# Matmul with batch norm on one core: a seventh raw row block, a fixed order of the tasks, and gamma's negation on GpSimd

## The chip, the cores and the metric

One core of a Trainium2 chip runs the kernel. The metric is the device time of one execution in microseconds, the median over several runs. The core has a matmul engine (TensorE, PE), a vector engine (VectorE, DVE), a scalar engine (ScalarE, ACT), a general engine (GpSimd, POOL) and a queue engine (SyncE, SP) that issues transfers. Each engine takes its own instructions in order, and they wait for each other through semaphores.

## The reference

```python
batch, m, k, n = 16, 512, 1024, 768
y = np.matmul(x, weight)                          # 8192 rows x 768 columns, all float32
mean = np.mean(y, axis=(0, 1), keepdims=True)     # per column
var = np.var(y, axis=(0, 1), keepdims=True)
y_norm = (y - mean) / np.sqrt(var + eps)
return (gamma * y_norm + beta).astype(np.float32)
```

Every output needs the mean and the variance of its column over all 8192 rows. So nothing of a column can be stored before all of its rows have been multiplied.

## The kernel before

The 8192 rows are cut into 16 chunks of 512 rows (`c`, C = 16), the 768 columns into 6 tiles of 128 (`nt`, NT = 6). x comes in through GpSimd's transfer queue as bfloat16 (L403), is turned by VectorE's 32x32 transposes (L428, L435), and for some chunks is also copied into a plain layout `x_pl` by ScalarE or VectorE (L547).

The first two column tiles are computed with rows on the partitions (L510, and L814 for the last two chunks). Their statistics are sums of the values and of the squares (L659 to L672), merged at L795 and L800 and summed over the partitions by a small matmul (L871). Their output is written in rows: VectorE multiplies (L937), GpSimd or VectorE adds the shift (L942), SP stores (L946). Chunks 14 and 15 of these tiles go through a TensorE transpose (L1074) instead.

The other four tiles are computed with columns on the partitions (L575, and L753 for the last chunk of the last tile). A unit is a matmul group over half of the depth, four matmuls; two units fill one of the eight banks of PSUM. The bank is free when VectorE has taken its statistics (L711) and ScalarE has copied it to SBUF (L715). For the third tile (nt = 2) ScalarE makes both sums itself from chunk 4 on (L720, L724). When a tile has all of its chunks, it is finished: total on ScalarE (nt = 2 alone, L980 to L986), variance on VectorE (L976), root on ScalarE (L990), then scale and shift per column (for nt = 2 L1001 on VectorE and L1004 to L1006 on ScalarE, with the negated gamma; for others L993 to L997).

An output block is two chunks of a tile, 1024 rows x 128 columns. Since it lies with columns on the partitions, it must be turned. There are three ways:

- `xact` (tiles 2 and 3): normalise in place (L1023 on ScalarE for nt = 2, L1026 on VectorE for nt = 3), transpose by a DMA that SP issues (L1220), convert to float32 on ScalarE (L1232), store (L1202).
- `pe` (tile 4): normalise, transpose on TensorE (L1044, single transposes put between the matmuls of later units), copy out on ScalarE (L1210), store (L1202).
- raw: the block is transposed by DMA before its statistics are known (L1106), and finished in rows: the scale and shift columns are spread along the rows (L1141, L1142 on VectorE, L1145 on GpSimd or ScalarE, L1158 on ScalarE), VectorE multiplies (L1174), GpSimd adds (L1178), SP stores (L1182). `RAW` names these blocks by tile and first chunk. Blocks of chunks 0 to 3 are transposed right behind the last load of x, ahead of the first store; the others later.

The last tile's 16 chunks are normalised on VectorE (L1348), transposed on TensorE (L1044), copied by ScalarE (L1361) and stored (L1364) after everything else. Their scale comes from L1308 to L1324. The first chunk is split into two quarters of a block for its stores.

The order of all this is made by a planner when the program is built. Each piece of work is a `Task` with a due time, the engines it may run on with assumed durations, what it depends on, and which buffers it takes or uses. `arrange` (L122) keeps a clock for each engine, takes the engine that can begin first, and gives it the ready task with the earliest due time. A unit of four matmuls may host single transposes of a block. Buffers are placed in the same pass, so the order also decides which earlier use a buffer has to wait for. The tasks are then emitted in that order, which fixes the order of instructions on each engine.

```python
RAW = {2:(0,2),3:(0,),4:(0,2,4)}                        # of L278
seq(nc.vector.tensor_scalar(ngamma, gamma_sb, -1.0, None, op0=ALU.mult))     # L964
ng = task(S, dve(0.1), negate_gamma, [affine, sr], True)                     # L966
```

Of the kernel before, what the change touches and what calls it, by code (L numbers as in the profile page):

```python
# [97 lines left out]
class Wires:  # L98
# [8 lines left out]
    def ready(self, queue):  # L107
        lanes = self.lanes[queue]
        return 0.0 if len(lanes) < self.LANES else lanes[-self.LANES]
# [9 lines left out]
        return t, land  # L119


def arrange(tasks, turns, log=None):  # L122

    free = {e: 1.25 for e in ("PE", "DVE", "ACT", "POOL", "SP")}
    wires = Wires()
    port = {"DVE": 0.0, "POOL": 0.0}
    left = sorted(tasks, key=lambda t: t.prio)
    order = []  # L130
    SEM, LOOK = 0.06, 0.2

    def ready(t):
        if t.after is not None and t.after.end is None:
            return None
        r = 0.0
        for d in t.deps:
            if d.end is None:
                return None
            r = max(r, d.end + SEM + t.slack)  # L140
        kept = [(s.pool, s.pool.mark()) for s in t.takes] if len(t.takes) > 1 else []
        fits = True
        for s in t.takes:
            p = s.pool.place(s)
            if p is None:
                fits = False
                break
            r = max(r, p[0] + SEM)
            if kept:
                s.pool.take(s, p[1])  # L150
        for pool, mark in reversed(kept):
            pool.reset(mark)
        if not fits:
            return None
        if t.dma:
            r = max(r, wires.ready(list(t.engines)[0]))
        return r

    def start_of(t, r, e):

        b = max(r, free[e])
        if e == "DVE" and t.lock:
            b = max(b, port["POOL"])
        elif e == "POOL" and not t.dma:
            b = max(b, port["DVE"])
        return b

    while left:
        seen = [(t, ready(t)) for t in left]
        first = {}  # L170
        for t, r in seen:
            if r is not None:
                for e in t.engines:
                    b = start_of(t, r, e)
                    if e not in first or b < first[e]:
                        first[e] = b
        if not first:
            raise RuntimeError(f"nothing can begin: {[(t.prio, t.emit) for t in left[:8]]}")
        e = min(first, key=lambda k: first[k])
        best = None  # L180
        for t, r in seen:
            if r is not None and e in t.engines and start_of(t, r, e) <= first[e] + max(LOOK, t.look):
                if best is None or t.prio < best[1]:
                    best = start_of(t, r, e), t.prio, t
        start, _, t = best
        for s in t.takes:
            s.pool.take(s, s.pool.place(s)[1])
        occ, lat = t.engines[e]
        t.hosted = []
        if t.hosts:  # L190
            room = t.hosts
            for u, r in seen:
                if u in turns and r is not None and r <= start + 0.3 and room >= 1:
                    n = min(room, turns[u][0])
                    if turns[u][0] == turns[u][1]:
                        places = [s.pool.place(s) for s in u.takes]
                        if any(p is None or p[0] > start for p in places):
                            continue
                        for s in u.takes:
                            s.pool.take(s, s.pool.place(s)[1])  # L200
                        u.takes_done, u.takes = u.takes, []
                    t.hosted.append((u, n))
                    turns[u][0] -= n
                    room -= n
                    occ += 0.0555 * n
                    lat += 0.0555 * n
        if t in turns:
            occ = lat = 0.0555 * turns[t][0]
            lat += 0.2
            t.count = turns[t][0]  # L210
        free[e] = start + occ
        if e == "DVE" and t.lock or e == "POOL" and not t.dma:
            port[e] = start + occ
        t.end = start + lat
        if t.dma:
            free[e], t.end = wires.send(e, start, occ, t.dma, t.count)
        t.start, t.engine = start, e
        order.append(t)
        left.remove(t)
        for u, n in t.hosted:  # L220
            if turns[u][0] == 0:
                u.end = t.end + 0.2
                left.remove(u)
    return order


# [1 line left out]
def kernel(  # L228
# [9 lines left out]
    nc = tc.nc  # L238
# [3 lines left out]
    ALU = mybir.AluOpType  # L242
# [5 lines left out]
    P = 128  # L248
# [26 lines left out]
    PARTED, LATE, SINGLE = (4,5,7,8,9,10), (12,13,14,15), (2,3,6)  # L275
    MODE = {2:'xact',3:'xact',4:('pe',)*8}
    MODE = {nt: m if isinstance(m, tuple) else (m,) * (C // GY) for nt, m in MODE.items()}
    RAW, RAWADD, RAWDUE = {2:(0,2),3:(0,),4:(0,2,4)}, {2:'POOL',3:'POOL',4:'POOL'}, {2:14.0,3:8.0,4:8.0}  # L278
    RING = 3 * CH // 32 * KQ // 2
    ENG = {"ACT": nc.scalar, "DVE": nc.vector, "POOL": nc.gpsimd, "SP": nc.sync}  # L280

# [11 lines left out]
    def seq(bi):  # L293

        ins = bi.ins
        prev = last.get(ins.engine)
        if prev is not None:
            tc.add_manual_dep(
                ins, prev,
                mybir.DependencyInfo(mybir.DependencyClass.NoSync, mybir.DependencyReason.DATA),  # L300
                reason="order",
            )
        last[ins.engine] = ins.name
        return bi

    gamma_sb = singles.tile([P, NT], f32)
# [28 lines left out]
    ngamma = singles.tile([P, NT], f32)  # L335
# [17 lines left out]
    tasks, turns = [], {}  # L353
    banks, xts, ys, sqs, rings = Pool(8), Pool(XT), Pool(YB), Pool(SQ), Space(RING)

    def task(prio, engines, emit, deps=(), lock=False, **kw):
        t = Task(prio, engines, emit, deps, **kw)
        t.lock = lock
        tasks.append(t)
        return t  # L360

    def dve(occ):
        return {"DVE": (occ, occ + 0.09)}
# [4 lines left out]
    def pool(occ):  # L368
        return {"POOL": (occ, occ + 0.05)}
# [70 lines left out]
    order = [("x", 0), ("w", 0, 2), ("x", 1), ("w", 2, 4)]  # L440
# [5 lines left out]
    t = 1.0  # L446
    affine = None
# [237 lines left out]
    def y_of(nt, c):  # L685
        return y_col.setdefault((nt, c // GY), Slot(ys))
# [174 lines left out]
    S = clock[0]  # L861
# [61 lines left out]
    sr = task(U + 0.1, dve(0.35), shift_rows, [sc], True)  # L923
# [32 lines left out]
    k = 0  # L956
# [4 lines left out]


    def negate_gamma(eng):
        seq(nc.vector.tensor_scalar(ngamma, gamma_sb, -1.0, None, op0=ALU.mult))  # L964

    ng = task(S, dve(0.1), negate_gamma, [affine, sr], True)  # L966

    def finish_tasks(nt):
        deps = [col_end[nt, c][0] for c in range(C)]
# [61 lines left out]
    def turn_block(prio, nt, m0, count, deps, uses):  # L1031

        bank = Slot(banks)
        todo = []

        def step():
            if not todo:
                o_ps = psum.tile([P, count, P], bf16, tag="b")
                bank.tile = o_ps
                for s in range(count):  # L1040
                    c, i = divmod(m0 // P + s, RT)
                    todo.append((o_ps[:, s], y(nt, c)[:, i * P:(i + 1) * P]))
            dst, src = todo.pop(0)
            seq(nc.tensor.transpose(dst, src, ident))  # L1044

        def emit(eng):
            for _ in range(emit.task.count):
                step()

        emit.step = step  # L1050
        t = task(prio, pe(0.0555 * count), emit, deps, takes=[bank], uses=uses)
        emit.task = t
        turns[t] = [count, count]
        return t, bank
# [213 lines left out]
    for nt in range(GA, NT - 1):  # L1268
# [10 lines left out]
        f = finish_tasks(nt)  # L1279
        start = clock[0] + 3.0  # L1280
# [58 lines left out]
    for c, r0, rows in ends:  # L1339
        due = E + 2.0 + 0.6 * c  # L1340
        n = max(rows // CH, 1)
# [13 lines left out]
        b, bank = turn_block(due + 0.6 * (n - 1), nt, m0, count, norms, [y_of(nt, c + i) for i in range(n)])  # L1355
# [7 lines left out]
        def store(eng, slot=slot, m0=m0, count=count):  # L1363
# [6 lines left out]
             uses=[slot])  # L1370

    order = arrange(tasks, turns)
    if "PLAN" in globals():
        PLAN.append(order)
# [37 lines left out]
```

## Time and profile before

| what | value |
|---|---|
| median of 3 runs | 206.29 us (206.23 to 206.86) |
| profiled execution, span from first to last instruction | 204.1 us |
| mean granted TensorE clock | 0.979 |
| first matmul on data (L510) | 12.14 us |
| last matmul of the last tile (L753), end in the chain of waits | 186.6 us |
| first transpose of a raw block issued (L1106) | 100.08 us |
| first store issued (L946) | 109.10 us |
| first store of the last tile issued (L1364) | 189.31 us |
| eleven stores of the last tile, issue from the first to the end of the last | 10.56 us |
| L1174, raw product on VectorE | 6, mean 1.21 us |
| L1178, raw sum on GpSimd | 6, mean 2.48 us |
| L1232, conversion on ScalarE | 13, mean 1.06 us |
| L1220, DMA transpose, on SP's queue | 13, median 1.70 us |
| L964, gamma's negation on VectorE | 1, 0.164 us |

A row of the groups gives line, engine, operation, written and read tile with the shape, the count, the busy time, the mean of one instruction in ns, and the idle time of the engine before it with what ended it. In a line of the timeline stand start, duration, engine, line and operation. In a line of the windows stand, after the stretch, its length, then the busy time and the count for PE, weight loads, DVE, ACT and POOL, then the granted clock, the DMA share and GB/s. A line of the waits has the waiting instruction, what ended the wait, the sum in us, how often, and the longest.

### The profile page before, as it was taken

Reading aid. Unit: us, or ns where it says so; the run is one execution under the profiler, and the core shown is the slowest. Engines: PE = TensorE matmul, PEld = TensorE weight load, DVE = VectorE, ACT = ScalarE, POOL = GpSimd, SP = SyncE. Lnnn points to the kernel's source line nnn. Section 1 sums busy time; section 2 is a strip of 40 time slices with the busy share of each in tenths; the row PEclk is TensorE's granted clock in tenths of the full one; section 3 lists DMA queues with packets and bytes.
Section 4 is the critical chain, followed back from the end, with each engine's and each line's share of the span. In section 5 each row is a group of like instructions: output and inputs, shape, how many; then the busy total and the mean of one; then the engine's idle time right before and its main releaser. Section 6 shows DMA issues by size and latency. Waiting matters only on the chain.

```text
span 204.1 us, 3510 instructions
## 1 busy us (share of the span) xinstructions
PE 189.3 (93%) x1210; PEld 114.5 (56%) x1210; DVE 159.3 (78%) x250; ACT 146.2 (72%) x260; POOL 124.1 (61%) x150
## 2 busy tenths in 40 slices
PE   7969999999999999999999999999999999997900
PEld 3457554657488888777865444444444445544600
DVE  4031879999999999969989998987999878657900
ACT  2001461368989999899978766999998959956950
POOL 7776954877499989997403999389613312940000
PEclk9999999999999999999999999999999999999965
DMA  4999999999999999999686899899999999999998
GB/s 71 172 199 196 176 196 196 196 197 197 190 193 197 197 196 196 196 197 195 103 181 200 297 339 336 248 301 328 295 322 227 336 303 274 347 343 310 310 347 253
DMA packets 98562, 48.74 MB, mean 239 GB/s; under 512 B 24304, under 2 KB 98032, under 8 KB 98544
## 3 DMA queue, kind: packets, MB, share of 16 engines
q0 software_dynamic: 34624, 18.36, 65.5%
q1 hardware_dynamic: 63920, 30.16, 52.6%
q8 instruction: 9, 0.15, 0.3%
q14 instruction: 9, 0.07, 0.1%
HBM read 36.71 MB, written 25.17 MB: 303 GB/s over the span
## 4 chain that ended last, share of the span: by engine, by line
PE 86%; ACT 3%; DMA 3%; POOL 2%; issue 1%; ACTq 0%; DVE 0%; POOLq 0%
PE y_ps L575 54%; PE y_ps L510 24%; PE y_ps L814 4%; ACT o_sb L1361 3%; DMA ring<-in_x_dram 3%; PE o_ps L1044 1%; POOL ring L403 1%; POOL w_sb L387 1%; PE y_ps L753 1%; PE a_ps L903 1%; PE o_ps L1074 0%; ACTq L1407 0%; PE idle_ps L591 0%; PE tot_ps L871 0%; ACT ring L1252 0%
## 5 line engine op out<-in xcount | busy, mean ns | idle before, releaser
L575 PEld LDWEIGHTS <-w_sb 128*128 128x128 bf16 x520 | 50.3, 97 | 57.6
L575 PE MATMUL y_ps<-xT_sb,w_sb 128*128 128x512 bf16 (+1 forms) x272 | 59.3, 371 | 0.0
L575 PE MATMUL y_ps<-x_pl,w_sb 128*128 128x512 bf16 x248 | 57.4, 379 | 0.0
L403 POOL DMA_DIRECT2D ring<-in_x_dram x76 | 47.2, 626 | 14.4 <-DMA ring<-in_x_dram 5.5
L510 PE MATMUL y_ps<-w_sb,xT_sb 128*128 128x256 bf16 x448 | 50.6, 273 | 1.7 <-DMA ring<-in_x_dram 1.6
L510 PEld LDWEIGHTS <-xT_sb 128*128 128x128 bf16 x448 | 43.5, 98 | 9.4 <-DVE xT_sb L435 2.9
L435 DVE STREAM_TRANSPOSE xT_sb<-ring 128x1024 f32<-128x1024 f32 (+1 forms) x29 | 31.2, 1111 | 14.1 <-DMA ring<-in_x_dram 13.9
L711 DVE BATCH_NORM_STATS2 stats<-y_ps 128x6 f32<-128x512 f32 x46 | 30.9, 687 | 7.7 <-PE y_ps L575 7.2
L715 ACT CAST y_sb<-y_ps 128x512 bf16<-128x512 f32 x51 | 29.0, 593 | 10.4 <-DVE stats L711 6.3
L547 ACT COPY x_pl<-xT_sb 128x1024 bf16<-128x1024 bf16 x32 | 32.8, 1063 | 1.7 <-DVE xT_sb L435 1.7
L942 POOL TENSOR_TENSOR ring<-ring,sum 128x1024 f32<-128x1024 f32 (+1 forms) x11 | 23.8, 2188 | 14.9 <-ACT y_ps L724 10.9
L659 ACT ACTIVATE sq_sb<-y_ps 128x512 f32<-128x512 f32 x28 | 16.3, 610 | 16.2 <-PE y_ps L510 15.9
L666 POOL TENSOR_TENSOR sum<-sum,sq_sb 128x512 f32<-128x512 f32 x20 | 25.6, 1278 | 3.0 <-ACT sq_sb L659 1.7
L662 DVE TENSOR_TENSOR sum<-y_ps,sum 128x512 f32<-128x512 f32 x28 | 18.9, 675 | 6.3 <-ACT sq_sb L659 5.3
L672 ACT CAST y_sb<-y_ps 128x512 bf16<-128x512 f32 x28 | 16.3, 594 | 8.2 <-DVE sum L662 8.0
L1178 POOL TENSOR_TENSOR ring<-ring,sum 128x1024 f32<-128x1024 f32 x6 | 14.8, 2477 | 9.8 <-issue 8.5
L937 DVE TENSOR_TENSOR ring<-y_sb,a_ps 128x1024 f32<-128x1024 bf16 (+1 forms) x16 | 16.7, 1079 | 0.1
L1044 PE MATMUL o_ps<-ident,y_sb 128*128 128x128 bf16 x104 | 13.1, 221 | 1.6 <-DVE y_sb L1348 1.5
L1232 ACT CAST ring<-ring 128x1024 f32<-128x1024 bf16 x13 | 13.8, 1063 | 0.6 <-DMA ring<-y_sb 0.6
L1145 POOL COPY sum<-sum 32x256 f32<-32x256 f32 (+1 forms) x17 | 5.8, 340 | 13.4 <-DVE sum L1142 6.5
L428 DVE STREAM_TRANSPOSE xT_sb<-ring 128x2048 bf16<-128x2048 bf16 x6 | 13.5, 2290 | 0.1
L591 PE MATMUL idle_ps<-idle_sb 128*128 128x512 f32 x18 | 9.6, 688 | 1.5 <-DVE idle_sb L316 1.5
(104 smaller groups left out, 153.7 us busy)
## 6 DMA issues: line engine op xcount, KB each, us to landing
out_dram<-ring SPq DMA_DIRECT2D x37, 512.0 KB, 3.4
ring<-in_x_dram POOLq DMA_DIRECT2D x52, 256.0 KB, 8.8
out_dram<-o_sb SPq DMA_DIRECT2D x6, 512.0 KB, 4.7
ring<-in_x_dram POOLq DMA_DIRECT2D x16, 128.0 KB, 5.9
w_sb<-in_weight_dram POOLq DMA_DIRECT2D x8, 192.0 KB, 6.2
out_dram<-ring SPq DMA_DIRECT2D x6, 256.0 KB, 3.0
ring<-in_x_dram POOLq DMA_DIRECT2D x4, 192.0 KB, 7.8
out_dram<-o_sb SPq DMA_DIRECT2D x3, 256.0 KB, 2.5
```

The lines of the kernel that those rows point to most:

```text
L403: bi = seq(nc.gpsimd.dma_start(x_bf[32 * i:32 * i + 32], src[:, :, KQ * i:KQ * (i + 1)]))
L435: seq(nc.vector.transpose(dst, src[:, :, jw0:jw1]))
L510: seq(nc.tensor.matmul(y_ps[:, s], x_of(c, jw, e, t * P, (t + 1) * P), w_sb[:, jw, e, 0:NA], start=(s == 0 and jw == 0 and e == 0), stop=( ...
L547: seq(nc.scalar.copy(dst, pairs) if eng == "ACT" else ENG[eng].tensor_copy(dst, pairs))
L575: seq(nc.tensor.matmul(y_ps, w_sb[:, jw, e, nt * P:(nt + 1) * P], moving(c, jw, e, q0 * QR, q1 * QR, parted), start=(jw == 0 and e == 0 an ...
L659: seq(nc.scalar.activation(sq_sb[:, 0:n], slot.tile[:, 0:n], AF.Square))
L662: seq(nc.vector.tensor_add(sum1, slot.tile[:, 0:n], sum1))
L666: seq(ENG[eng].tensor_add(acc, acc, state["sq"][:, 0:n]))
L711: seq(nc.vector.bn_stats(dst, slot.tile))
L715: seq(nc.scalar.copy(y(nt, c), slot.tile))
L937: seq(nc.vector.tensor_mul(slot.o, y_row[c].y[:, s0:s1], aff[0][:, None, :].to_broadcast([P, n, NA])))
L942: seq(ENG[eng].tensor_add(slot.o, slot.o, row[:, None, :].to_broadcast([P, n, NA])))
```

## The change

1. `RAW` gets block (3, 2): the rows of chunks 2 and 3 of the fourth column tile are now transposed raw and finished in rows, as (3, 0) was before.
2. The planner no longer chooses. A table `ORDER` names every task by its number in the order of creation, with the letter of its engine (P, V, A, G, S), and after a plus sign the blocks whose transposes a matmul unit hosts and how many of each. `arrange` walks the table, keeps its clocks for the placing of buffers, and raises an error when a task is not ready.
3. Gamma's negation runs on GpSimd, and depends on the load of gamma alone.

```diff
+ORDER = (
+    "G0 P59 G3 G8 A9 G4 G7 V1 V2 P60 G10 P61 P62 P63 P64 P65 V5 V6 P66 G12 P67 P68 P69 P70 P71 G14 P76 A72 "
...
+    "V643 V657 V683 V661 V675 V644 G645 G646 P685+658.4 P686+658.4 P689+662.4 P690+662.3 P678+662.1 A684 "
...
+    "A760 A775 S739 S766 S771 S743 S781 S776 S761 "
+)
...
-    left = sorted(tasks, key=lambda t: t.prio)
+    left = tasks
...
-    while left:
-        seen = [(t, ready(t)) for t in left]
...
-        e = min(first, key=lambda k: first[k])
...
+    NAMES = {"P": "PE", "V": "DVE", "A": "ACT", "G": "POOL", "S": "SP"}
+    for word in ORDER.split():
+        word, _, riders = word.partition("+")
+        t, e = left[int(word[1:])], NAMES[word[0]]
+        r = ready(t)
+        if r is None:
+            raise RuntimeError(f"out of order: {word}")
+        start = start_of(t, r, e)
...
+        for rider in riders.split(",") if riders else ():
+            i, n = rider.split(".")
+            u, n = left[int(i)], int(n)
...
-    RAW, RAWADD, RAWDUE = {2:(0,2),3:(0,),4:(0,2,4)}, {2:'POOL',3:'POOL',4:'POOL'}, {2:14.0,3:8.0,4:8.0}
+    RAW, RAWADD, RAWDUE = {2:(0, 2),3:(0, 2),4:(0, 2, 4)}, {2:'POOL',3:'POOL',4:'POOL'}, {2:14.0,3:8.0,4:8.0}
...
     def negate_gamma(eng):
-        seq(nc.vector.tensor_scalar(ngamma, gamma_sb, -1.0, None, op0=ALU.mult))
-
-    ng = task(S, dve(0.1), negate_gamma, [affine, sr], True)
+        seq(nc.gpsimd.tensor_scalar(ngamma, gamma_sb, -1.0, None, op0=ALU.mult))
+
+    ng = task(S, pool(0.3), negate_gamma, [affine])
```

What the table makes of the order, read from the two built programs:

- Up to the last chunk of x the engines' orders agree; the first differences stand where the row sums are merged (L795, L871).
- SP issues six raw transposes ahead of the first store instead of five, then the row stores and those of chunks 14 and 15 alternate.
- TensorE has the same matmuls and transposes. Eight column matmuls stand between the transpose blocks of chunks 14 and 15 that stood behind them; units of different chunks alternate more often; the hosted transposes are spread otherwise.
- At the finish of the third tile VectorE runs three L937 ahead of the aggregate L976 (two and an L711 before), then the spreading copies L1141, L1142 and one more L937 ahead of the next L711, and ScalarE runs the root, L1004 to L1006 and three L1023 ahead of the first L715 of the next tile. Before, one L715 stood ahead of the root, and one behind each L1023.
- GpSimd runs the negation behind the first two L942, the copies L1318 to L1320 behind the last L942, and the four small copies L1145 of the fifth tile that ScalarE ran.
- In the last tile the stores L1364 begin with chunks 1 and 2 (a half each) and 15, and the two quarters of chunk 0 come as number five and eight.

More of the change, by code (lines that the diff above doesn't have):

```diff
@@ L128, in arrange @@
     port = {"DVE": 0.0, "POOL": 0.0}
-    left = sorted(tasks, key=lambda t: t.prio)
+    left = tasks
     order = []
-    SEM, LOOK = 0.06, 0.2
+    SEM = 0.06
     def ready(t):
@@ L166, in start_of @@
         return b
-    while left:
-        seen = [(t, ready(t)) for t in left]
[L170 to L178, printed above, removed]
-        e = min(first, key=lambda k: first[k])
[L180 to L185, printed above, removed]
+    NAMES = {"P": "PE", "V": "DVE", "A": "ACT", "G": "POOL", "S": "SP"}
[6 more added lines that the diff above has]
+        start = start_of(t, r, e)
         for s in t.takes:
@@ L189, in arrange @@
         t.hosted = []
[L190 to L206, printed above, removed]
+        for rider in riders.split(",") if riders else ():
+            i, n = rider.split(".")
+            u, n = left[int(i)], int(n)
+            if turns[u][0] == turns[u][1]:
+                for s in u.takes:
+                    s.pool.take(s, s.pool.place(s)[1])
+                u.takes_done, u.takes = u.takes, []
+            t.hosted.append((u, n))
+            turns[u][0] -= n
+            occ += 0.0555 * n
+            lat += 0.0555 * n
         if t in turns:
@@ L218, in arrange @@
         order.append(t)
-        left.remove(t)
         for u, n in t.hosted:
@@ L222, in arrange @@
                 u.end = t.end + 0.2
-                left.remove(u)
     return order
```

36 rows, old and new, of the table ORDER are left out of this document.

## The prediction

> **What bounds the kernel now.** I read the page's busy rows first, then the waits of TensorE, then the chain of waits, then the last stage in windows, and last one stretch of ScalarE and VectorE where the change moves most.
>
> From the page:
> ```profile
> span 204.1 us, 3510 instructions
> ...
> PE 189.3 (93%) x1210; PEld 114.5 (56%) x1210; DVE 159.3 (78%) x250; ACT 146.2 (72%) x260; POOL 124.1 (61%) x150
> ```
> The waits of TensorE (us in total, times, longest), all that there are:
> ```profile
> PE y_ps L510 <- DMA ring<-in_x_dram: 1.6, 1, 1.6
> PE o_ps L1044 <- DVE y_sb L1348: 1.5, 1, 1.5
> PE idle_ps L591 <- DVE idle_sb L316: 1.5, 1, 1.5
> ```
> Two of these lie in the first 12.14 us, the third after the last column statistics. Between them TensorE never waits; the chain of waits shows it (start, us, what):
> ```profile
> 110.40 58.94 PE y_ps L575 x269
> ...
> 184.80 1.81 PE y_ps L753 x16
> ...
> 189.60 4.74 ACT o_sb L1361 x6
> ```
> So from 12.1 to 186.6 the time is matmul after matmul, 0.219 us each in the long run (58.94 / 269). After that the sixth column tile, 4 MB, must be stored, in eleven stores whose first is issued at 189.31. The windows of that stage (last number GB/s, the one before it the DMA share):
> ```profile
> 174.00:180.00 6.00, 6.00 (x40) 3.10 (x38) 4.15 (x6) 5.52 (x8) 4.71 (x3) 1.00 1.16 349
> ...
> 186.00:188.00 2.00, 1.06 (x14) 0.81 (x11) 1.25 (x6) 1.61 (x5) 0.00 (x0) 1.00 1.08 324
> 188.00:190.00 2.00, 1.37 (x16) 0.87 (x16) 1.96 (x7) 1.49 (x5) 0.00 (x0) 1.00 0.86 258
> 190.00:192.00 2.00, 2.00 (x28) 1.39 (x25) 2.00 (x8) 2.00 (x4) 0.00 (x0) 1.00 0.90 271
> 192.00:202.00 10.00, 2.09 (x27) 1.35 (x24) 1.64 (x6) 4.67 (x6) 0.00 (x0) 0.68 1.15 347
> ```
> 347 GB/s is this kernel's full rate: 4 MB take 12.1 us. The transfers are full from 192 on. Only 188 to 192 has a hole, (347 - 258 + 347 - 271) x 2 / 347 = 0.95 us worth, while old stores run out and the new ones start. Thus the end is: end of matmuls, a short chain of statistics, twelve microseconds of drain. A change that leaves the matmuls alone can win at most this hole, and loses whatever it makes TensorE wait.
>
> **The change, part by part.** The profiled execution takes 204.1 us in its span, 2.2 below the 206.29 median; I carry the 2.2 over. Up to about 98 us the built instruction order of both kernels is the same on every engine, so nothing differs there.
>
> Row block 2 of the fourth column tile. It loses a norm (VectorE L1026, 0.54), a DMA transpose in the store stage (L1220, 1.70 at the median on SP's queue) and a ScalarE conversion (L1232, 1.06). It gains a raw transpose ahead of the first store (L1106), a VectorE product (L1174, 1.21) and a GpSimd sum (L1178, 2.4). VectorE +0.67, ScalarE -1.06, GpSimd +2.4. None of it is on the path: VectorE waits for matmuls 7.2 us in eight waits at L711, and GpSimd is idle 6.04 us before 152.33 and 6.46 before 161.40. Without that cover the price is the 0.67 or the 2.4. The five early transposes run from 100.08 to 106.94; a sixth, 1.37 more, ends at 108.3, before the first store of 109.10, in a window (108 to 110) in which DMA moves 4 GB/s. Two row-store issues and all stores stand behind it on SP; cost 0, at most 1.37 for the first store, which lies 77 us before the end. One transpose fewer among the stores: 1.0 to 1.7 us of DMA, which is worth something only if old stores still block the last drain; the hole at 188 says they do not. I take 0.
>
> Negation of gamma (VectorE L964, 0.164): now a GpSimd instruction behind the first two sums of row output. GpSimd shows no negation; its nearest rows are 0.18 (a copy of one column, L1318) and 0.228 (32x64, L1145). Its reader, L1004, starts at 126.47, some 13 us later: 0. In the new order L1318 to L1320 move back behind the row sums, but their reader L1324 runs at 187.93: 0. The gathering copies of the fifth tile go from ScalarE (4 x 0.242) to GpSimd (4 x 0.228), behind idle time of 6.26 us: 0.
>
> The searched order. This is the part that can cost. TensorE issues the same matmuls, so its work is equal; the question is where it now waits for a bank. One place stands out, the finish of the third column tile. ScalarE and VectorE there now:
> ```profile
> 123.86 0.29 ACT L986 ACTIVATE sums<-sums 128x1 f32<-128x1 f32 x1
> ...
> 126.47 0.29 ACT L1004 ACTIVATE nscale<-rstd,ngamma 128x1 f32<-128x1 f32 x1 [1.09 <-DVE rstd L1001]
> ...
> 127.26 1.24 ACT L1023 ACTIVATE y_sb<-y_sb,shift,scale 128x1024 bf16<-128x1024 bf16 x1
> 128.41 0.56 ACT L715 CAST y_sb<-y_ps 128x512 bf16<-128x512 f32 x1
> ```
> ```profile
> 121.45 2.34 DVE L937 TENSOR_TENSOR ring<-y_sb,a_ps 128x1024 f32<-128x1024 bf16 x2
> 123.87 0.70 DVE L711 BATCH_NORM_STATS2 stats<-y_ps 128x6 f32<-128x512 f32 x1
> 124.48 0.26 DVE L976 BATCH_NORM_AGGREGATE mv<-sums 128x2 f32<-128x27 f32 x1
> ```
> In the new order the aggregate L976 stands behind a third L937, and ScalarE runs three L1023 before its first L715 of the next tile, where now one L715 stands ahead of the root and one after every L1023. Counting: the third L937 starts at 123.75 to 124.1 and lasts 1.13 to the next start; L976 0.26; then root 0.30, reciprocal 0.15, L1004 to L1006 0.79 (126.47 to 127.26), hand-overs 0.06; then 3 x 1.145 and the L715's 0.58. The first bank is free at 130.6 to 130.9 (VectorE's L711 for it comes after the spreading copies and one L937, some 2 us after L1006, at 129.5, and so in time). TensorE: the two transpose blocks end at 110.40 now and come 8 matmuls later (1.75) in the new order; 84 matmuls at 0.219 follow, so the 85th, which waits for that L715, is due at 112.15 + 18.4 = 130.55. Stall: 0.05 to 0.35. If the third L937 must also wait for its ring block, the longest such wait in the trace, 0.7 (L1174 on a store), comes on top: up to 1.05. A gain is excluded, for the matmuls run without a gap now. I take 0.25, in the middle of the counted values. Everything behind it, VectorE's statistics and the whole drain, moves by the same.
>
> The tail's order. The first store of the last tile is now a quarter (128x2x128) and becomes a half: its norm 405 ns instead of 342, two transposes more at 0.055, its copy 616 instead of 376: 0.41 later, at 189.7. But it brings twice the bytes, 0.74 us of transfer, and the next copies follow every 0.48, so the transfers then stay full. Bounds: -0.54 (the hole of 0.95 closes and 0.41 is paid) and +0.41 (nothing closes). The hole ends because the copies come slowly and not through idle transfers at one point, so I take a value nearer the late start: +0.15.
>
> Sum: 206.29 + 0.25 + 0.15 = 206.7 us (a span of 204.5).
>
> A row on contention: one L1178 lasts 2.83 at most against 2.35 at least, and it is the one that a VectorE copy L547 of 0.96 (others 0.68) overlaps at 143.11. So such a meeting costs each side 0.3 to 0.5. The Trainium skill, "SBUF — State Buffer", section "Who interferes with whom", says more: whichever of the two starts first holds the shared port pair for its whole instruction and the other fully blocks. The trace agrees only in part, since neither was held back for the other's whole length. By the row the added GpSimd sum costs nothing on the path; by the rule it can cost the second rival below.
>
> **The rivals.**
> Slower through the bank: the stall at L575 takes its upper value, 1.05, and the tail its upper 0.41: 207.75. It decides from the point where the third L937 starts later than 124.1. For it: the trace shows L937 and L942 back to back there and no free VectorE time; against: TensorE has eight banks and waits nowhere now.
>
> Slower through the port: a VectorE instruction on the way to a matmul or a bank waits for one whole GpSimd sum, 2.4, less the 0.9 that VectorE has in hand on average (7.2 / 8): 206.7 + 1.5 = 208.2. For it: GpSimd has one sum more; against: L1026 stays within 506 to 625 ns in twelve cases.
>
> Faster through the drain: the order of the last stores and the transpose taken out of the store stage close the hole and TensorE never stalls: 206.29 - 0.95 = 205.35. For it: the transfers are full at 174 to 188 and from 192 on; against: the hole comes from late supply, and the first store comes later.
>
> Nothing happens: both costs are hidden, 206.3.
>
> **How the numbers follow.** 0.3% is 0.62 us, about what a measurement of this kernel tells from no change. Forecast 206.7 (206.3 to 207.1) 0.42; nothing 0.08; bank 0.30; port 0.08; faster 0.12. Of the forecast 0.06 lies above 206.91. So faster 0.12, same 0.44, slower 0.44. The range goes from 205.7, inside the faster case, to 207.75, the bank's full price; the port and most of the faster case, under 0.2, stay out.
>
> **What would show it.** TensorE's waits after the change: one line with L575 behind ScalarE, near 131 us, of 0.1 to 0.4 (forecast), none (nothing), about 1 (bank). Six early L1106 ending before 108.5; first row store no later than 109.5. Seven L1174, seven L1178, twelve L1220. L1004 not waiting for GpSimd. The first last-tile store 0.6 to 0.7 later than 189.31, the windows from 191 on at 347 GB/s. The prediction is wrong if the last L753 ends before 186.4, or if TensorE waits at a second place between 98 and 186.

## The result, and the profile after

The changed kernel takes 213.06 us (median of six runs, 211.05 to 214.27), the kernel before beside it 206.12 (six runs, 205.84 to 206.86): ratio 1.0307, 95% interval 1.0273 to 1.0342. By the medians it is slower by 6.9 us; the ratio, which is formed without the longest run (214.27), stands for 6.3. The prediction was 206.7, in a range from 205.7 to 207.75. The profiled execution is that longest one (span 212.5). It lost 1.07 us ahead of 98 us, where both kernels have the same instructions: the matmuls at L838 begin at 97.94, those of before (L814) at 96.87, since TensorE waited 0.5 longer for the first block of x and 0.5 for a transposed one. Line numbers of the changed kernel are those of before plus 24 (L1141 is L1165, L547 L571, L1026 L1050, L942 L966, L1178 L1202).

The busy rows of the page after:
```profile
span 212.5 us, 3508 instructions
...
PE 190.8 (90%) x1210; PEld 115.6 (54%) x1210; DVE 167.6 (79%) x248; ACT 144.4 (68%) x256; POOL 128.9 (61%) x156
```
VectorE has two instructions fewer and works 8.3 us longer (159.3 before). TensorE's waits after (us in total, times, longest):
```profile
PE y_ps L599 <- ACT y_sb L739: 4.3, 4, 2.1
PE o_ps L1068 <- DVE y_sb L1372: 2.6, 3, 1.6
PE y_ps L534 <- DMA ring<-in_x_dram: 2.1, 1, 2.1
...
PE o_ps L1068 <- DVE y_sb L1050: 1.2, 1, 1.2
```
The first and the last are new: TensorE now waits for banks and for products in the middle of the span. The last matmuls L777 end at 194.69, those of L753 before at 186.62: 8.07 of the 8.4 us between the spans were lost ahead of that point, 1.07 of them ahead of 98 us. The chain of waits had 126 pieces before, one of them 58.94 us long; now it has 309. Those that are VectorE's and far too long (start, us, what):
```profile
128.13 3.67 DVE sum L1165 x2
...
148.53 2.38 DVE x_pl L571
...
162.07 2.35 DVE x_pl L571
...
167.95 2.96 DVE y_sb L1050 x2
```
The windows at the first hole and in the last stage:
```profile
132.00:136.00 4.00, 1.89 (x8) 0.66 (x7) 4.00 (x6) 1.72 (x2) 2.09 (x7) 1.00 1.22 255
...
188.00:190.00 2.00, 2.00 (x14) 1.05 (x13) 1.70 (x2) 1.01 (x1) 0.58 (x2) 1.00 1.15 342
190.00:192.00 2.00, 2.00 (x14) 1.01 (x12) 1.30 (x2) 1.16 (x3) 2.00 (x1) 1.00 1.14 344
192.00:202.00 10.00, 7.39 (x73) 5.83 (x71) 9.00 (x28) 8.79 (x18) 0.13 (x1) 0.85 0.99 297
```
From 132 to 136 TensorE is busy 1.89 of 4 us while VectorE is never idle. The stretch ahead of it, first VectorE, then GpSimd, then ScalarE, then TensorE (start, us, what):
```profile
127.36 0.16 DVE L1025 RECIPROCAL rstd<-std 128x1 f32<-128x1 f32 x1 [0.36 <-ACT std L1014]
128.13 1.31 DVE L1165 COPY sum<-scale 128x32 f32<-128x32 f32 x1 [0.61 <-ACT scale L1029]
129.36 2.42 DVE L1165 COPY sum<-shift 128x32 f32<-128x32 f32 x1
...
133.09 1.28 DVE L735 BATCH_NORM_STATS2 stats<-y_ps 128x6 f32<-128x512 f32 x2
```
```profile
122.36 9.38 POOL L966 TENSOR_TENSOR ring<-ring,sum 128x1024 f32<-128x1024 f32 x4 [0.92 <-DVE ring L961]
```
```profile
133.81 0.58 ACT L739 CAST y_sb<-y_ps 128x512 bf16<-128x512 f32 x1 [1.90 <-DVE stats L735]
```
```profile
134.45 2.17 PE L599 MATMUL y_ps<-xT_sb,w_sb 128*128 128x512 bf16 x8 [2.07 <-ACT y_sb L739]
```
Two copies of 32 columns, 0.17 us each where nothing meets them, last 1.31 and 2.42. They stand under four GpSimd sums that follow one another; the second copy ends at 131.78, the last sum at 131.74. The statistics L735, the copy L739 that empties the bank, and TensorE come after them, in this order. The same happens at 148.44, first VectorE, then GpSimd:
```profile
148.44 2.47 DVE L571 COPY x_pl<-xT_sb 128x1024 bf16<-128x1024 bf16 x1
```
```profile
145.03 2.75 POOL L1202 TENSOR_TENSOR ring<-ring,sum 128x1024 f32<-128x1024 f32 x1 [2.21 <-DVE ring L1198]
148.00 2.36 POOL L1202 TENSOR_TENSOR ring<-ring,sum 128x1024 f32<-128x1024 f32 x1 [0.22 <-DVE ring L1198]
```
This L571 lasts 2.47 against 0.66, and the sum runs to 150.36. So it is at 162.07 (2.35, sum from 161.50 to 163.87) and at 168.33 (an L1050, the normalisation, of 2.58 against 0.53, sum from 168.03 to 170.62). Each time the VectorE instruction begins inside a sum and ends behind the sum's end: by 0.04 for the two small copies, and by 0.55, 0.55 and 0.29, about its own work, for the large ones. Not every VectorE instruction is held back. The products L961 and the statistics L735, which read PSUM, last as long under a sum as without one (L961 1.21 in nine cases under a sum, 1.18 to 1.21 in three without; L735 0.68 to 0.70 and 0.67 to 0.70). No wait is listed for these times, since the delay lies inside the instruction.

I add up, for each profile, by how much the VectorE copies and tensor-scalars after 98 us that overlap a GpSimd instruction exceed their unmet lengths (L1165 0.17, L571 0.66, L1050 0.53, L1088 0.41; 0.1 or more counted). Before: 0.8 us. After: 10.5 us, in seven instructions.

### The profile page after: what moved, and what is told of

It is laid out like the page before. It is cut to its first block, busy times and chain, and to the rows that moved or that the text cites. A ratio compares the mean times of both kernels' runs of the same rounds, so it can differ in the third digit from the quotient of the medians.

```text
span 212.5 us, 3508 instructions
## 1 busy us (share of the span) xinstructions
PE 190.8 (90%) x1210; PEld 115.6 (54%) x1210; DVE 167.6 (79%) x248; ACT 144.4 (68%) x256; POOL 128.9 (61%) x156
## 4 chain that ended last, share of the span: by engine, by line
PE 36%; DVE 26%; DMA 14%; issue 7%; ACT 7%; POOL 5%; SPq 2%; DVEq 0%; ACTq 0%; POOLq 0%
PE y_ps L599 17%; DMA ring<-in_x_dram 12%; PE y_ps L534 10%; DVE ring L961 5%; DVE stats L735 4%; PE y_ps L838 3%; DVE x_pl L571 3%; PE o_ps L1068 3%; POOL ring L427 3%; DMA out_dram<-ring 3%; DVE y_sb L1050 3%; DVE sum L1165 2%; DVE xT_sb L459 2%; DVE ring L966 2%; DVE sum L686 2%
## 5 line engine op out<-in xcount | busy, mean ns | idle before, releaser
L599 PEld LDWEIGHTS <-w_sb 128*128 128x128 bf16 x520 | 50.0, 97 | 61.6 <-issue 5.8
L599 PE MATMUL y_ps<-xT_sb,w_sb 128*128 128x512 bf16 (+1 forms) x272 | 61.4, 371 | 2.3 <-ACT y_sb L739 2.2
L599 PE MATMUL y_ps<-x_pl,w_sb 128*128 128x512 bf16 x248 | 58.8, 379 | 2.1 <-ACT y_sb L739 2.1
L534 PEld LDWEIGHTS <-xT_sb 128*128 128x128 bf16 x448 | 43.5, 98 | 10.5 <-DVE xT_sb L459 4.1
L739 ACT CAST y_sb<-y_ps 128x512 bf16<-128x512 f32 x51 | 28.6, 592 | 12.7 <-DVE stats L735 10.8
L571 ACT COPY x_pl<-xT_sb 128x1024 bf16<-128x1024 bf16 x33 | 33.9, 1058 | 1.7 <-DVE xT_sb L459 1.7
L735 DVE BATCH_NORM_STATS2 stats<-y_ps 128x6 f32<-128x512 f32 x46 | 29.8, 682 | 4.9 <-PE y_ps L599 4.9
L966 POOL TENSOR_TENSOR ring<-ring,sum 128x1024 f32<-128x1024 f32 (+1 forms) x11 | 23.7, 2179 | 15.1 <-ACT sum L939 11.3
L1202 POOL TENSOR_TENSOR ring<-ring,sum 128x1024 f32<-128x1024 f32 x7 | 17.1, 2450 | 12.3 <-DVE ring L1198 12.3
L1169 POOL COPY sum<-sum 32x64 f32<-32x64 f32 (+1 forms) x21 | 7.6, 363 | 15.1 <-DVE sum L1166 14.3
L961 DVE TENSOR_TENSOR ring<-y_sb,a_ps 128x1024 f32<-128x1024 bf16 (+1 forms) x16 | 16.6, 1074 | 0.0
L1256 ACT CAST ring<-ring 128x1024 f32<-128x1024 bf16 x12 | 12.5, 1056 | 1.2 <-DMA ring<-y_sb 1.2
L1068 PEld LDWEIGHTS <-y_sb 128*128 128x128 bf16 x104 | 8.5, 111 | 6.1 <-DVE y_sb L1372 3.4
```

What stands on the lines that cost most here:

```text
L534: seq(nc.tensor.matmul(y_ps[:, s], x_of(c, jw, e, t * P, (t + 1) * P), w_sb[:, jw, e, 0:NA], start=(s == 0 and jw == 0 and e == 0), stop=( ...
L571: seq(nc.scalar.copy(dst, pairs) if eng == "ACT" else ENG[eng].tensor_copy(dst, pairs))
L599: seq(nc.tensor.matmul(y_ps, w_sb[:, jw, e, nt * P:(nt + 1) * P], moving(c, jw, e, q0 * QR, q1 * QR, parted), start=(jw == 0 and e == 0 an ...
L735: seq(nc.vector.bn_stats(dst, slot.tile))
L739: seq(nc.scalar.copy(y(nt, c), slot.tile))
L961: seq(nc.vector.tensor_mul(slot.o, y_row[c].y[:, s0:s1], aff[0][:, None, :].to_broadcast([P, n, NA])))
```

## The experiments

The theory, from these rows: VectorE copies and GpSimd sums exclude each other, and the table lets them meet where the planner kept them apart (port theory, after `port`, in which the planner keeps the time until which the other engine is at such work). Rivals: the order itself holds the banks too long (bank order); the added parts cost by themselves (parts); GpSimd's work costs by its length and late stores (length). In the table, "excess" is the sum just described, "L753 ends" the end of the last matmuls of the sixth tile (L777 in kernels with the table), both of the profiled execution. Kernels with a name in t_ come from the changed kernel, the others from the one before.

| kernel | median us | ratio to before, 95% | excess | L753 ends |
|---|---|---|---|---|
| changed | 213.06 | 1.0273 to 1.0342 | 10.5 | 194.69 |
| p_both | 207.99 | 1.0086 to 1.0125 | 0.1 | 186.73 |
| p_raw | 207.94 | 1.0079 to 1.0114 | 0.0 | 186.68 |
| t_small | 206.06 | 0.9999 to 1.0021 | 0.6 | 186.20 |
| b_small | 205.65 | 0.9971 to 1.0003 | 0.2 | 186.58 |
| t_spread_act | 212.16 | 1.0261 to 1.0310 | 7.1 | 192.19 |
| t_all_act | 211.66 | 1.0244 to 1.0287 | 3.1 | 192.36 |
| t_small_raw | 209.99 | 1.0158 to 1.0222 | 5.2 | 190.10 |
| p_blind | 209.66 | 1.0153 to 1.0212 | 4.9 | 188.51 |
| t_split4 | 213.70 | 1.0361 to 1.0410 | 7.2 | 193.04 |
| t_split2 | 209.44 | 1.0161 to 1.0202 | 6.0 | 189.84 |
| t_spread_early | 210.93 | 1.0200 to 1.0283 | 7.4 | 191.75 |
| b_split4 | 208.76 | 1.0129 to 1.0166 | 0.2 | 188.72 |
| t_order1 | 207.85 | 1.0062 to 1.0106 | 2.4 | 188.41 |
| t_order2 | 207.43 | 1.0040 to 1.0087 | 0.6 | 187.57 |

**The parts without the table.** p_raw is the kernel before with the raw block; p_both has the negation on GpSimd too.
```diff
-    RAW, ... = {2:(0,2),3:(0,),4:(0,2,4)}, ...
+    RAW, ... = {2:(0,2),3:(0,2),4:(0,2,4)}, ...
-        seq(nc.vector.tensor_scalar(ngamma, gamma_sb, -1.0, None, op0=ALU.mult))
-    ng = task(S, dve(0.1), negate_gamma, [affine, sr], True)
+        seq(nc.gpsimd.tensor_scalar(ngamma, gamma_sb, -1.0, None, op0=ALU.mult))
+    ng = task(S, pool(0.3), negate_gamma, [affine])
```


> The kernel before with the raw block and the negation on GpSimd, but with the planner's own order in place of the table. Port theory (the loss comes from VectorE copies that meet GpSimd sums, which the planner keeps apart and the table does not): 205.5 to 207, the seventh L1174 and L1178 there, VectorE's L547 rows within 0.65 to 0.97 and L1141 within 0.16 to 0.7. Rival parts (the raw block and its GpSimd sum cost by themselves): 209 or more. Rival bank order says nothing here against the port theory: it too expects about 206.

> The kernel before with the raw block alone, the planner's own order. Port theory: 205.5 to 207. Rival parts: 2.4 us more of GpSimd on the path, 208 or more.


Both take 2.0 us more, between what the two theories expected, and by neither's way: no copy is long (excess 0.0 and 0.1), and TensorE's main work ends within 0.1 us of before. The 2 us are in the drain. The windows of p_raw, DMA rate last:
```profile
170.00:180.00 10.00, 10.00 (x72) 5.43 (x70) 7.04 (x13) 9.32 (x16) 4.03 (x5) 1.00 0.86 244
```
Before moves 319 GB/s there; (319 - 244) x 10 / 347 = 2.2 us of transfer that must come after the end. The waits of SP's queue from 150 to 190 name what was late, a conversion that ScalarE had behind other work (3.3 in total, at most 1.0, before):
```profile
SPq L1202 <- ACT ring L1232: 8.2, 6, 2.8
```
So the raw block makes the planner find another order, with stores that come late. The block need not cost this: t_small below has it too, though with its sums cut short, and loses nothing. The negation adds nothing (207.99 against 207.94).

**The sums cut short.** t_small cuts every L966 and L1202 on GpSimd to 128 elements of a partition and leaves out the rest of the shift; b_small is its control. The edit at L1202, that at L966 is alike:
```diff
-            seq(ENG[eng].tensor_add(slot.o, slot.o, row[:, None, :].to_broadcast([P, n, P])))
+            w = 1 if eng == "POOL" else n
+            seq(ENG[eng].tensor_add(slot.o[:, :w], slot.o[:, :w], row[:, None, :].to_broadcast([P, w, P])))
```


> The changed kernel, order table and all, with every GpSimd sum (L966, L1202) cut to 128 elements of a partition: the rest of the shift is not added. Port theory: the VectorE copies have nearly nothing left to wait for, L571 falls from a mean of 1.24 to below 0.8, L1050 from 0.72 to below 0.6, L1165 from 0.55 and 0.93 to below 0.4, and the time falls to 205.5 to 207.5. Rival bank order (the sequence of ScalarE and VectorE work is what makes TensorE wait): TensorE still waits at L599 behind ScalarE for 3 to 5 us and the time stays at 210 or more.

> The control: the kernel before with the same cut of its GpSimd sums. Port theory: its copies met next to nothing, so the time stays within 0.6 us of the kernel before. Rival: if this kernel falls by several us too, the sums cost by their length and not by meeting VectorE.


t_small falls by 7.0 us to the time of before, b_small stays. The table's order is unchanged in t_small, and no L599 waits any more: bank order falls. From the first L838 to the end of the last L777 TensorE needs as long as before, to within 0.02 us, where the changed kernel needed 7.0 more. Two of its VectorE groups (busy, mean ns), which were 1242 and 925 in the changed kernel:
```profile
L571 DVE COPY x_pl<-xT_sb 128x1024 bf16<-128x1024 bf16 x7 | 4.9, 707 | 0.2 <-ACT x_pl L571 0.2
L1167 DVE COPY sum<-shift 128x32 f32<-128x32 f32 x3 | 0.5, 176 | 0.1
```
It also shortens GpSimd's work by 32.5 us (96.4 against 128.9), so length still stands. t_small_raw cuts L1202 alone.


> The changed kernel with the seven sums L1202 alone cut to 128 elements of a partition (the rest of that shift is left out); the row-output sums L966 stay at 2.4 us. Port theory: the meetings of L571 and L1050 with L1202 go (about 6 us of VectorE), the meeting of L1165 with L966 at 128 to 132 stays, 208 to 210.5, and L1165 still shows copies of over 1 us. Rival length: the L966 sums are the long ones early on, 9 of 16 remain, so the gain is at most half of 7 us and no VectorE row changes.


The time, 209.99, and the rows are as the port theory had them: the L1165 copies still last 1.31 and 2.44, the L571 and L1050 that met L1202 are short. Its gain, 3 us, would have fitted the rival length too (at most half of 7); it is the rows that speak against that.

**Copies moved to ScalarE.** t_spread_act moves L1165 only, t_all_act the L571 copies too.
```diff
-                seq(nc.vector.tensor_copy(wide[:, quadrant(i)], src[:, nt:nt + 1].to_broadcast([P, 32])))
+                seq(nc.scalar.copy(wide[:, quadrant(i)], src[:, nt:nt + 1].to_broadcast([P, 32])))
```


> The changed kernel, every GpSimd sum at full length, but the six small spreading copies (L1165) moved from VectorE to ScalarE. Port theory: the meeting at 128 to 132 us (3.5 us of VectorE beyond the 0.17 each) is gone, the meetings of L571 and L1050 with L1202 stay, so the time falls by 1.5 to 3 to between 209.5 and 211.5. Rival length (the sums cost because each is 2.4 us long and its store comes late, not because it meets VectorE): nothing got shorter, so 212.5 or more. Rival bank order: ScalarE gets six more instructions at the very place where TensorE waited behind it, so 213 or more.

> As the last one, and the seven VectorE copies L571 moved to ScalarE too (7 x 1.06 us more there). Port theory: only the meetings of L1050 and L1088 are left (about 3 us of VectorE), the time falls to 207 to 210. Rival bank order or ScalarE as the bound: 7.4 us more on ScalarE makes TensorE wait longer behind it, 213 or more. Rival length: 212.5 or more.


Both gain less than expected. In t_spread_act the copies stood behind two products L1047 on ScalarE, and VectorE's next instruction waited as long as it had been blocked:
```profile
129.49 0.25 DVE L1166 STREAM_TRANSPOSE sum<-sum 128x64 f32<-128x64 f32 x1 [3.52 <-ACT sum L1165]
```
t_all_act has little excess left (3.1) and ScalarE busy 10.00 of 10 us from 150 to 160 and again from 160 to 170, and TensorE still waits 3.1 us at L599 behind ScalarE: by these rows the loss had only changed its engine, which was not tried further. t_spread_early puts the copies of the third tile directly behind L1030.
```diff
+            if nt in RAW:
+                for i, src in enumerate((scale, shift)):
+                    seq(nc.scalar.copy(sum1[:, NA + 32 * i:NA + 32 * (i + 1)], src[:, one].to_broadcast([P, 32])))
```


> The changed kernel with the two spreading copies of the third tile (L1165 there) on ScalarE and, unlike in t_spread_act, directly behind L1030 and ahead of the L1047 products, where t_spread_act had them behind two of these so that VectorE waited 3.5 us for ScalarE in place of GpSimd. Port theory: VectorE's transposition L1166 runs by 127.5, TensorE's idle time at 130 to 140 falls from 2.3 us to below 0.5, the later meetings stay: 209.5 to 211.5. Rival bank order (the sequence itself lets TensorE wait there): it still waits 1 us or more at 130 to 134.


Now TensorE is idle 0.23 us from 130 to 140 (9.77 busy of 10; 7.73 in the changed kernel), and the time is 210.93, inside the port theory's range.

**The planner made blind.** p_blind is the kernel before, where no task has the mark by which the planner keeps VectorE's copies out of GpSimd's work.
```diff
-        t.lock = lock
+        t.lock = False
```


> The kernel before with one line changed: the planner no longer knows that some VectorE instructions and GpSimd's exclude each other (t.lock = False). All instructions, sizes and engines stay as the planner chooses. Port theory: its order now lets them meet; L547, L1026 and L1141 show single rows of over 1.2 us that end with a GpSimd sum, and the time rises to 208 to 213. Rival (such meetings cost each side only 0.3 to 0.5, as the prediction took): 206 to 207.


An L547 of 2.55, another of 1.28 and an L1026 of 2.24 appear, each ending 0.29 to 0.55 after a sum's end; L1141 stays short. The rows bear the theory out, the time, 209.66, does not measure it: TensorE lost 1.9 us at 81.72 to a late input transpose and only 0.2 behind the long copies. As far as TensorE goes, three meetings far apart were absorbed. Another 1.9 us came in the drain (19.32 us from the end of the last L753 to the end of the span, 17.45 before), and what caused that was not taken apart.

**The sums in pieces.** Each sum as four instructions (t_split4, control b_split4) or two (t_split2). The edit for the raw sums and four pieces, the others are alike:
```diff
-            seq(ENG[eng].tensor_add(slot.o, slot.o, row[:, None, :].to_broadcast([P, n, P])))
+            m = n // 4 if eng == "POOL" else n
+            for i in range(0, n, m):
+                part = slot.o[:, i:i + m]
+                seq(ENG[eng].tensor_add(part, part, row[:, None, :].to_broadcast([P, m, P])))
```


> The changed kernel, all its work at full size, but each long GpSimd sum (L966, L1202) issued as four instructions of 256 elements of a partition, about 0.71 us each by 2.19 ns an element and 0.15 fixed (2.39 and 1.27 for 1024 and 512): GpSimd works 0.45 us longer for each sum. Port theory (a VectorE copy waits for the GpSimd instruction that runs, and only for that one): the longest L571, L1050 and L1165 fall from 2.4 to below 1.5, their sums by 5 us or more, and the time falls to 207 to 210. Rival length (the sums cost by their length and late stores): GpSimd is longer, so 213 or more. Port theory with GpSimd keeping the port between its own instructions: rows stay at 2.4 or more, 213 or more.

> The same with two instructions for each sum (1.27 us each). Port theory: the longest VectorE copies fall to about 1.3 to 1.9, the time between the changed kernel and t_split4, 208.5 to 211.5. Rivals as there: 213 or more.

> The control: the kernel before with its sums in four instructions each. Port theory: it has no long meetings to shorten, and GpSimd has idle time for the 0.45 us more of each sum: 205.8 to 207. If it falls below 205.5 the short meetings of before (L547 at 0.96) cost more than I think.


Two pieces do what was expected: the longest copy is 1.49, the time 209.44. Four pieces do not (213.70), and in one place alone, where it is the last case of the expectation: GpSimd keeps its turn between its own instructions. VectorE, GpSimd and TensorE there:
```profile
127.21 5.76 DVE L1174 COPY sum<-scale 128x32 f32<-128x32 f32 x1 [0.60 <-ACT scale L1038]
```
```profile
123.28 9.64 POOL L975 TENSOR_TENSOR ring<-ring,sum 128x256 f32<-128x256 f32 x14
```
```profile
135.71 5.75 PE L599 MATMUL y_ps<-xT_sb,w_sb 128*128 128x512 bf16 x19 [5.02 <-ACT y_sb L739]
```
A copy of 0.17 us lasted 5.76, through eight ends of sums, until GpSimd had none left at 132.92. TensorE then waited 5.02, which is most of the 7.9 us that this kernel loses. Everywhere else its copies are short (at most 1.20). The control moved as well, by 3.0 us and not to between 205.8 and 207, with next to no meeting (excess 0.2): in its profile, with GpSimd busy 130.7 us against 124.1, TensorE waits 1.4 us for a normalisation (L1035, L1026 of before) and the drain is 1.1 longer. So length is not free, and the share of the two in t_split4 stays open.

**Order alone.** t_order1 and t_order2 start from t_spread_early, with whole sums, and move six and seven words. The second:
```diff
-  A418 V339 V387 V345
+  A418 V387 V339 V345
-  P600 V461 V579 G376 ... V464 V525 A580 A522 V583
+  P600 V579 A580 V583 V461 G376 ... V464 V525 A522
-  V549 V588 ... G550 ... V590 V546 V572 V560
+  V588 ... V590 V572 V560 V549 V546 G550
```
V579, V583 and V588 to V590 are copies L571, V387 an L1088, V572 and V560 L1050; V339 is a product L961, and V461, V549 and V546 are products L1198, whose GpSimd sum a copy behind them would meet; G550 is such a sum, and A580 a ScalarE copy that must be named ahead of V583.


> The changed kernel as in t_spread_early, all sums whole, with five VectorE words of the table moved so that a copy goes ahead of the product L1198 whose GpSimd sum it met (one L1088, two L571, and two L1198 put behind an L571 and two L1050). The work and the engines are those of t_spread_early; only the order differs. Port theory: the L571 of 2.7 us at 145 and the L1050 of 2.6 at 165 fall to 0.7 and 0.53, TensorE waits less than 2 us between 98 and 186, and the time falls from 210.9 to 206.5 to 209. Rival length (GpSimd's sums cost by being long, wherever VectorE stands): 210 or more, for every sum still is 2.4 us.

> As t_order1, but the product L1198 of row block 2 of the fourth column tile goes behind all three L571 copies of that stretch and both L1050, so that no copy can meet its sum either. Port theory: no VectorE copy or L1050 after 98 us lasts over 1.5 us; 206 to 208.5, unless the later store opens a hole in the drain, which would show as less than 300 GB/s at 170 to 186. Rival length: 210 or more.


207.85 and 207.43, in the port theory's ranges. In t_order1 one L571 still met a sum (2.54). In t_order2 the groups and TensorE's waits read:
```profile
L1053 DVE TENSOR_SCALAR y_sb<-y_sb,scale,shift 128x1024 bf16<-128x1024 bf16 x11 | 5.7, 543 | 0.0
L571 DVE COPY x_pl<-xT_sb 128x1024 bf16<-128x1024 bf16 x7 | 5.3, 761 | 1.8 <-ACT x_pl L571 1.8
```
```profile
PE y_ps L599 <- ACT y_sb L739: 0.7, 1, 0.7
```
Every sum is as long and as many as in the changed kernel, and 5.6 of the 7 us are gone by the medians (5.0 by the ratios). Some 2 us of this came with t_spread_early, the rest with the seven words. A copy that goes ahead of a product also reaches TensorE one product, 1.2 us, earlier, with or without a meeting. That part was not separated; but in t_small the copies stand behind the products as in the changed kernel, and it loses nothing by that. Of the 1.4 us left over the kernel before, 0.7 are this one bank wait, and the rest was not taken apart. No kernel that does the whole work is faster than the one before.

## Why the prediction was wrong

**The failed step is the last of the change, on contention.** It read from one row that a meeting costs each side 0.3 to 0.5, and took nothing for it. In its place the runs show that the VectorE instruction waits for all that is left of the sum, up to 2.4 us. The new order has seven such meetings with 10.5 us, and TensorE's matmuls end 7.0 later behind them. Three rows of before already said more, had I held them against GpSimd's. VectorE, then GpSimd, of the kernel before:
```profile
135.28 0.64 DVE L1141 COPY sum<-scale 128x32 f32<-128x32 f32 x1
...
143.11 0.96 DVE L547 COPY x_pl<-xT_sb 128x1024 bf16<-128x1024 bf16 x1
...
145.76 0.54 DVE L993 SCALAR_TENSOR_TENSOR tmp<-mv,gamma_sb 128x1 f32<-128x1 f32 x1
```
```profile
131.19 4.70 POOL L942 TENSOR_TENSOR ring<-ring,sum 128x1024 f32<-128x1024 f32 x2 [3.54 <-DVE ring L937]
...
141.10 5.19 POOL L1178 TENSOR_TENSOR ring<-ring,sum 128x1024 f32<-128x1024 f32 x2
```
The first copy, 0.47 too long, ends at 135.92, and the sums at 135.89. The second begins 0.41 ahead of the end of the first L1178 (2.41 from 141.10), and 0.41 + 0.55 is its 0.96; the next sum, listed from 143.46, is then 0.48 longer than the shortest, which fits a wait for this copy. The third, 0.16 long where nothing meets it, ends at 146.31, and that sum at 146.29; it is neither a copy nor a tensor-scalar and so not in the excess. All three waited for all that was left of a sum. What I took for the price of a meeting was a short remainder; the price is the remainder, from nothing to 2.4. The Trainium skill, "SBUF — State Buffer", section "Who interferes with whom", states for VectorE in its 2-port modes, which use the port pair that it shares with GpSimd, that the one that issues first holds this pair for its whole instruction and that the other fully blocks. I wrote that the trace agreed only in part; these rows agree in full, as do 2.47 and 2.35 after. The 5.76 of t_split4 does not: there sums that are listed as beginning after the copy went ahead of it. In which mode an instruction ran stands in no row.

**The port rival had the mechanism and the wrong count.** It priced one meeting at 1.5 us (2.4 less 0.9 in hand) and had a chance of 0.08. There were seven, with 10.5 us in all, and TensorE's end moved by 7.0 after 98 us. Its argument against, "L1026 stays within 506 to 625 ns in twelve cases", came from a kernel whose planner, by its own clocks, starts no copy while a GpSimd sum runs (`start_of` and `port`): the trace could not show what the order avoided. The table keeps `start_of` but cannot act on it; the order is fixed, and where the chip's times differ from the planned ones the copy goes into the sum.

**The bank stall (0.25).** The place was right, 131 us, the cause not: 2.07 there, because L735 "at 129.5, and so in time" came at 133.09, behind the two blocked copies. Without meetings the stall is 0 (t_small) or, with ScalarE spreading, 0.7 at most (t_order2). The upper value, 1.05, was the case of a late L937, not of a blocked copy.

**The raw block (0).** Its engines' sums were as counted, and so was the sixth transpose in the planner's order: six take 8.30 us in p_raw and end at 108.51 (108.3 forecast). In the table it waited 2.0 us for an L961 and the first row store left at 112.93, not by 109.5; in t_small it left at 110.60 and the kernel is as fast as before; the 112.93 was not tried by itself. That 2 us could come from the planner's reaction, as in p_raw, was not among my cases, nor did it count in this kernel.

**The negation and the gathering copies (0):** right; L1028 waits for VectorE's reciprocal alone (0.29).

**The tail's order (+0.15).** From the end of the last L753 or L777 to the end of the span: 17.45 us before, 17.80 after, 17.81 in t_small, 17.56 in t_order2. That is 0.35, 0.37 and 0.12 more, inside the bounds of -0.54 and +0.41. The first store of the last tile leaves 2.69 us behind L753 before and 3.09 behind L777 in t_small: 0.40, counted as 0.41. The hole did not close: it is at 196 to 200 now, with 279 and 241 GB/s (258 and 271 before, at 188 to 192). The 347 GB/s that I called the kernel's full rate is that of this stage; before moves 385 at 122 to 124.

**What would make it wrong** named a second wait of TensorE between 98 and 186. There are four at L599 alone.

Without the meetings the time lies in the stated range: t_small, all of the change with the sums cut short, measures 206.06 against 206.7, and t_order2, with whole sums, 207.43. That t_small is so near is in part luck, for its stall is 0 and not 0.25, its tail 0.37 and not 0.15, and it leaves out most of the sums.

## What to carry to other kernels

When an order made by a scheduler is replaced by a fixed one, list the rules that the scheduler enforced and look for each in the new order, with the measured durations; the old trace cannot show what a broken rule costs, since the rule kept it out. A blocked instruction is not idle: compare each instruction's longest with its usual length, and look at what runs on the other engine when it ends. In this kernel a short copy was best placed ahead of the instruction that starts the long sum on the other engine, rather than behind it.

## What was not expected of the hardware

A waiting VectorE copy did not always get its turn at the end of a GpSimd instruction. In the changed kernel and in t_split2 it did (the copy of 128.13 ends at 129.44, a sum at 129.40, while the next is listed from 129.37), in t_split4 it lost eight times running, 5.76 us. What decides it was not tried. The other way round GpSimd waits too: the L1202 that starts inside an L571 at 145.03 lasts 2.75, where the next, which begins inside no copy, lasts 2.36.
